# Copies of queries and keys within their own partitions: VectorE instead of transfers

## The chip, the cores and the metric

The kernel runs on one core of a Trainium2 chip. The metric is the device time of one execution in microseconds (us); lower is better. The engines of the core are TensorE (PE), VectorE (DVE), ScalarE (ACT), GpSimd (POOL) and SyncE (SP). SP issues all transfers (DMAs) of this kernel; the 16 DMA engines carry them out.

## The reference

The kernel computes a trunk of two layers over 2048 tokens of width 1024. Each layer normalizes its input, projects it to eight groups of 512 columns, runs two mixers side by side, gates and joins them, and projects back. The change concerns the queries and keys of the first mixer, chunked softmax attention with 8 heads of 64.

```python
def hybrid_layer(x, norm_gain, w_in, w_out, rel_bias, cos, sin):
    hn = rms_norm(x, norm_gain)
    proj = hn @ w_in.astype(hn.dtype)
    aq, ak, av, ag, rq, rk, rv, rg = jnp.split(proj, cuts, axis=-1)
    ya = chunked_rel_attention(aq, ak, av, rel_bias)      # 8 heads x 64, own chunk and 8 before
    yr = chunkwise_retention(rq, rk, rv, cos, sin)        # 4 heads x 128, recurrent state
    y = jnp.concatenate([ya * silu(ag), yr * silu(rg)], axis=-1)
    return x + y @ w_out

# in chunked_rel_attention, per chunk of 64 queries and its band of 576 keys:
    scores = jnp.einsum("bnqhd,bnkhd->bnhqk", qc, kb) * (dh ** -0.5)
    p = jax.nn.softmax(scores + bias, axis=-1)
    out = jnp.einsum("bnhqk,bnkhd->bnqhd", p, vb)
```

After the two layers comes a final RMS norm.

## The kernel before

**Numbers in two halves.** Matmul operands are f16. To keep more than f16's precision, a value is held as an upper half (the value rounded to f16) and a lower half (what the rounding left). ScalarE makes the upper half, VectorE the lower half by one subtraction. A projection is three matmul passes: upper by upper, upper by lower, lower by upper.

**Blocks.** A layer has four head groups `s` (two attention heads and one retention head each) and four stretches `n` of 512 tokens: 16 blocks a layer, 32 in all. A block first runs `dense_T` and then `dense_V`. `dense_T` computes four sections `j`, each 128 columns by 512 tokens with the columns on the partitions, in 24 matmuls of 512 columns (line 870; in the very first block lines 851 and 870): j = 0 attention queries, 1 attention keys, 2 and 3 the queries and keys of retention. `dense_V` computes four tiles of 128 tokens (line 891) with values and gates. Beside these matmuls run the attention and retention of the block before, in small portions between groups of eight matmuls: score matmuls (lines 939 and 940), the reduction of the scores on VectorE (943), exponential and upper half on ScalarE (946, 948), the lower half on POOL (949), a transposing transfer of both halves, `pT`, by SP (951), the product with the values (959 to 961), and retention products (999). The output projection of each layer (1289) follows after its 16 blocks.

**Queries and keys.** For j = 0 ScalarE writes the upper half of the queries into `qq[:, 0]` (line 767), and `q_rest` writes the lower half into `qq[:, 1]` (line 770). `qq` has the first head of the group on partitions 0 to 63 and the second on 64 to 127. The score matmuls contract over 128 partitions: on the key side 64 hold the upper half and 64 the lower half of one head, so each head's queries have to stand twice, on both halves of the partitions. `st.q[:, hx]` is that tile for head `hx`. `q_rest` fills it with four transfers (line 774), each of 64 partitions by 1024 f16 values. For j = 1 the same happens with `kk` (lines 781, 784): `k_rest` makes `st.k` by four transfers (lines 785 to 788) of 64 partitions by 512 values. In each set, two transfers keep the partitions of their source, and two move to the other half.

**Buffers.** `st.q` has two buffers and `st.k` three; `qq` and `kk` have one each, and these are used again in the same block for the rotation of the retention keys and queries. Dense products land in two PSUM tiles in turn (`psD`), the scores in one (`psS`), and the small products in four (`psR`).

**Order.** The order on PE, ACT, DVE and POOL is the order in which the program issues its instructions. It is written out by hand: `run` steps a block's matmuls in rounds, and each step may put work off by a number of rounds (`later`, with the table `PLACES`; ties go by `RANK`); `soon` puts `q_rest` and `k_rest` off in that way. In the very first block `soon` runs them at once, and the list `FIRST` orders the whole start: there the two evacuations stand directly ahead of the step `Vsc2`, which computes the scale (lines 1425 to 1433) for two sections of the V weights; ScalarE then converts these (1495) and VectorE makes their lower halves (1498). `PLAN` places the preparation of later tokens: squares, gain product on POOL (333, 1382), rounding on ScalarE (303), subtraction on VectorE (309), and two transposing transfers (312, 313). Of SP's queue only the start has a written order; after it, a planner places the transfers by estimated costs and due times.

Of the kernel before, what the change touches and what calls it, by code (L numbers as in the profile page):

```python
# [93 lines left out]
def hybrid_trunk(ctx: ExitStack, tc: tile.TileContext, x, pos, gain, gcol, w_in, w_out, rel, fgain,  # L94
# [9 lines left out]
    act, dve, pool, pe, sp = nc.scalar, nc.vector, nc.gpsimd, nc.tensor, nc.sync  # L104
# [580 lines left out]
    def later(k, fn, kind=None):  # L685
        if kind is not None:
            k = G(kind, k)
        if k <= 0:
            fn()
            return  # L690
        deferred.append([k, fn, kind])
# [16 lines left out]
    def dense_T(l, s, n, g, st):  # L708
# [12 lines left out]
        def soon(fn):  # L721
            if first:
                fn()
            else:
                later(1, fn, fn.__name__)

        def first_rotation(j, ps, rot):
            if j == 2:
                st.rq = rot
                later(1, tab_load)  # L730
                own = rot[:, 1:3].rearrange("p a c -> p (a c)").bitcast(F32)
            else:
                st.rk = rot
                own = b1.tile([P, 512], F32, tag="qq", name=f"raw{nm}")
            st.swp = []

            def cosine():
                dve.scalar_tensor_tensor(out=own, in0=ps, scalar=2.0 ** -16, in1=st.tabc, op0=ALU.mult, op1=ALU.mult)

            def sine(half):  # L740
                if half == 0:
                    st.swp = b1.tile([P, 512], F32, tag="swp", name=f"swp{nm}_{j}")
                i_, o_ = slice((1 - half) * 64, (2 - half) * 64), slice(half * 64, half * 64 + 64)
                dve.scalar_tensor_tensor(out=st.swp[o_], in0=ps[i_], scalar=-2.0 ** -16, in1=st.tabs[i_], op0=ALU.mult,
                                         op1=ALU.mult)

            def tokens():
                st.kt = b1.tile([P, KT, P], F16, tag="ktok", name=f"kt{nm}")
                sp.dma_start_transpose(out=st.kt, in_=rot.rearrange("p a c -> p (a c)"))

            d = 2 * j
            later(d, cosine)
            later(d, lambda: sine(0))
            later(d + 1, lambda: sine(1))
            later(d + 2, lambda: dve.tensor_tensor(own, own, st.swp, op=ALU.add))
            later(d + 3, lambda: act.activation(rot[:, 0], own, AF.Copy))
            later(d + 4, lambda: dve.tensor_tensor(rot[:, 1], own, rot[:, 0], op=ALU.subtract))
            if j == 2:
                later(d + 5, lambda: act.activation(rot[:, 2], rot[:, 0], AF.Copy, scale=2.0 ** -11))
            else:  # L760
                later(d + 6, tokens)

        def evacuate(j, ps):
            if j == 0:
                st.q = b2.tile([P, 2, 2, 512], F16, tag="q", name=f"q{nm}")
                qq = b1.tile([P, 2, 512], F16, tag="qq", name=f"qq{nm}")
                act.activation(qq[:, 0, :], ps, AF.Copy, scale=2.0 ** -16)

                def q_rest():
                    dve.scalar_tensor_tensor(out=qq[:, 1, :], in0=ps, scalar=2.0 ** -16, in1=qq[:, 0, :], op0=ALU.mult,  # L770
                                             op1=ALU.subtract)
                    for hx in range(2):
                        for half in range(2):
                            sp.dma_start(st.q[half * 64:half * 64 + 64, hx], qq[hx * 64:hx * 64 + 64])

                soon(q_rest)
            elif j == 1:
                st.k = b3.tile([P, 2, 512], F16, tag="k", name=f"k{nm}")
                kk = b1.tile([P, 2, 512], F16, tag="swp", name=f"kk{nm}")
                kh, kl = kk[:, 0, :], kk[:, 1, :]  # L780
                act.activation(kh, ps, AF.Copy, scale=2.0 ** -16)

                def k_rest():
                    dve.scalar_tensor_tensor(out=kl, in0=ps, scalar=2.0 ** -16, in1=kh, op0=ALU.mult, op1=ALU.subtract)
                    sp.dma_start(st.k[0:64, 0, :], kh[0:64, :])
                    sp.dma_start(st.k[64:128, 1, :], kh[64:128, :])
                    sp.dma_start(st.k[64:128, 0, :], kl[0:64, :])
                    sp.dma_start(st.k[0:64, 1, :], kl[64:128, :])

                soon(k_rest)  # L790
            else:
                w = 5 - j
                rot = b2.tile([P, w, 512], F16, tag=f"rot{j}", name=f"rot{nm}_{j}")
                if first:
                    first_rotation(j, ps, rot)
                    return
                if j == 2:
                    raw = rot[:, 1:3].rearrange("p a c -> p (a c)").bitcast(F32)
                else:
                    raw = b1.tile([P, 512], F32, tag="qq", name=f"raw{nm}")  # L800
                act.activation(raw, ps, AF.Copy, scale=2.0 ** -16)

                def swap(rot=rot, raw=raw, j=j):
                    swp = b1.tile([P, 512], F32, tag="swp", name=f"swp{nm}_{j}")
                    sp.dma_start(swp[0:64, :], raw[64:128, :])
                    sp.dma_start(swp[64:128, :], raw[0:64, :])

                    def turned(out_, x_, y_, op):
                        return lambda: dve.tensor_tensor(out_, x_, y_, op=op)

                    def upper():
                        act.activation(rot[:, 0], raw, AF.Copy)

                    def lower():
                        dve.tensor_tensor(rot[:, 1], raw, rot[:, 0], op=ALU.subtract)

                    def third():
                        act.activation(rot[:, 2], rot[:, 0], AF.Copy, scale=2.0 ** -11)

                    def tokens():  # L820
                        st.kt = b1.tile([P, KT, P], F16, tag="ktok", name=f"kt{nm}")
                        sp.dma_start_transpose(out=st.kt, in_=rot.rearrange("p a c -> p (a c)"))

                    d = 4 if j == 2 and first else 3
                    later(d, turned(raw, raw, st.tabc, ALU.mult), None if first else f'ro0{j}')
                    later(d + 1, turned(swp, swp, st.tabs, ALU.mult), None if first else f'ro1{j}')
                    later(d + 2, turned(raw, raw, swp, ALU.add), None if first else f'ro2{j}')
                    later(d + 3, upper, None if first else f'ro3{j}')
                    later(d + 4, lower, None if first else f'ro4{j}')
                    if j == 2:  # L830
                        later(d + 5, third, None if first else 'ro52')
                    else:
                        later(11, tokens, 'tok')

                if j == 2:
                    st.rq = rot
                    swap()
                    if first:
                        later(1, tab_load)
                else:  # L840
                    st.rk = rot
                    later(2, swap, 'sw')

        if first:
            ps = [psD.tile([P, 512], F32, tag="dense", name=f"dT{nm}_{j}") for j in range(2)]
            for (j, a) in ((0, 0), (0, 1), (0, 2), (1, 0), (1, 1), (1, 2), (0, 3), (1, 3)):
                cs = slice(a * P, (a + 1) * P)
                m = 0
                for (w_, h_) in ((g.h, hh), (g.h, hl), (g.l, hh)):
                    for kt in range(KT):  # L850
                        pe.matmul(ps[j][:, cs], w_[:, j, kt, :], h_[:, kt, cs], start=(m == 0), stop=(m == 23))  # L851
                        m += 1
                yield
            for j in range(2):
                evacuate(j, ps[j])
                yield
# [696 lines left out]
    for l in range(DEPTH):  # L1553
        gO = [Grp(), Grp()]
        go = Grp()
        for s in range(NSW):
            g = grp(l, s)
            for n in range(NS):
                first = (l, s, n) == (0, 0, 0)
                if not first:  # L1560
                    st = states.setdefault((l, s, n), St())
                    dT = dense_T(l, s, n, g, st)
                else:
                    st = st0
# [129 lines left out]
```

## Time and profile before

| what | value |
| --- | --- |
| median of 3 runs | 2025.08 us (2023.61 to 2025.53) |
| the profiled execution | 2026.06 us |
| its span, first to last instruction | 2024.3 us |
| granted TensorE clock, mean | 0.998 |
| busy: PE, DVE, ACT, POOL | 1987.4, 1298.6, 1157.4, 464.6 us |
| DMA queue of the kernel, share of 16 engines | 67.5% |
| transfers into `st.q` | 128, median 2.4 us from issue to landing |
| transfers into `st.k` | 128, median 2.0 us from issue to landing |

How to read the lines below: a row of a timeline gives the start in us from the span's start, the duration in us, the engine, the line of the kernel, the operation, output and input tiles by name, the shape, and a count; in brackets stands the idle time of the engine just before, with what ended it. A row of waits gives who waited for whom, the total in us, how often, and the longest. "PEld" is the loading of weights into TensorE, "SPq" the issuing of a transfer by SP. A matmul row lasts longer than the distance to the next one, since matmuls are pipelined.

### The profile page before, as it was taken

The numbers are of one execution on the slowest core, as the hardware profiler recorded it, in microseconds if no ns is written. First come the engines' busy times: TensorE is split into PE (matmuls) and PEld (weight loads), VectorE is DVE, ScalarE is ACT, GpSimd is POOL, SyncE is SP. The second block draws the span as 40 slices with busy tenths as digits, with TensorE's granted clock in tenths as the row PEclk, the third lists the DMA queues.
The fourth block names the chain that finished last, engine by engine and source line by source line (L and its number), as shares of the span: only waits on it lengthen the run. The fifth ranks groups of instructions, "written<-read, shape, count | busy, mean of one in ns | idle before, by whom it ended". The sixth has DMA issues, their size and how long they took to land.

```text
span 2024.3 us, 39702 instructions
## 1 busy us (share of the span) xinstructions
PE 1987.4 (98%) x14006; PEld 1047.4 (52%) x14006; DVE 1298.6 (64%) x4014; ACT 1157.4 (57%) x2525; POOL 464.6 (23%) x521
## 2 busy tenths in 40 slices
PE   6999999999999999999999999999999999999998
PEld 5444555555555555544444555555555555555544
DVE  7777767566656665766655557665766676557543
ACT  7666765566666655655445556655665665456432
POOL 2443222222222222220001222222212222222100
PEclk9999999999999999999999999999999999999999
DMA  9698765466586754899973547554755776558874
GB/s 269 137 187 191 159 145 123 105 144 127 131 186 139 148 135 101 187 244 266 236 183 94 119 97 163 121 119 102 162 119 132 168 163 161 119 123 185 208 206 125
DMA packets 655385, 315.25 MB, mean 156 GB/s; under 512 B 468784, under 2 KB 612144, under 8 KB 655184
## 3 DMA queue, kind: packets, MB, share of 16 engines
q1 hardware_dynamic: 655184, 312.70, 67.5%
q8 instruction: 110, 1.80, 0.4%
q14 instruction: 91, 0.75, 0.1%
HBM read 123.26 MB, written 41.98 MB: 82 GB/s over the span
## 4 chain that ended last, share of the span: by engine, by line
PE 89%; DMA 4%; DVE 4%; issue 1%; ACT 1%; SPq 1%; POOL 0%; POOLq 0%; ACTq 0%; DVEq 0%
PE dT L870 31%; PE dV L891 30%; PE dO L1289 13%; PE r L999 4%; PE S L940 3%; PE S L939 3%; DMA pT<-pq 2%; PE o L959 2%; PE o L960 2%; PE o L961 2%; PE dT L851 1%; DVE sc L943 0%; DMA x_d<-hTl 0%; DMA yly<-rly 0%; DMA xa<-in_x_dram 0%
## 5 line engine op out<-in xcount | busy, mean ns | idle before, releaser
L949 POOL TENSOR_TENSOR pq<-sc,pq 128x640 f16<-128x640 f32 (+4 forms) x256 | 329.3, 1286 | 1169.8 <-issue 710.3
L946 ACT ACTIVATE sc<-sc,mq,cT 128x640 f32<-128x640 f32 (+4 forms) x256 | 218.4, 853 | 427.7 <-DVE mq L945 427.6
L891 PE MATMUL dV<-whV,hTh 128*128 128x512 f16 x1024 | 352.1, 380 | 0.9 <-DVE gt L909 0.9
L891 PE MATMUL dV<-wlV,hTh 128*128 128x512 f16 x1024 | 352.2, 380 | 0.0
L891 PE MATMUL dV<-whV,hTl 128*128 128x512 f16 x1024 | 352.1, 379 | 0.0
L870 PE MATMUL dT<-hTh,whT 128*128 128x512 f16 x1008 | 346.6, 379 | 0.8 <-DMA hTh<-hTl 0.8
L870 PE MATMUL dT<-hTl,whT 128*128 128x512 f16 x1008 | 346.6, 379 | 0.0
L870 PE MATMUL dT<-hTh,wlT 128*128 128x512 f16 x1008 | 346.6, 379 | 0.0
L943 DVE CUSTOM_DVE_ANT_0 sc<-S,bias 128x640 f32<-128x640 f32 (+4 forms) x256 | 188.7, 737 | 197.9 <-PE S L940 196.8
L891 PEld LDWEIGHTS <-hTh 128*128 128x128 f16 x2048 | 196.6, 98 | 209.7 <-DVE gt L909 1.9
L870 PEld LDWEIGHTS <-whT 128*128 128x128 f16 x2016 | 192.5, 98 | 199.0 <-DVE gt L909 1.3
L948 ACT ACTIVATE pq<-sc 128x640 f16<-128x640 f32 (+4 forms) x256 | 171.5, 670 | 8.1
L1289 PE MATMUL dO<-whO,yly 128*128 128x512 f16 (+2 forms) x456 | 171.2, 376 | 1.5 <-DMA yly<-rly 1.5
L1289 PE MATMUL dO<-whO,yhy 128*128 128x512 f16 (+2 forms) x456 | 171.5, 377 | 0.5 <-DMA yhy<-rhy 0.5
L1289 PE MATMUL dO<-wlO,yhy 128*128 128x512 f16 (+2 forms) x456 | 171.5, 377 | 0.0
L891 PEld LDWEIGHTS <-hTl 128*128 128x128 f16 x1024 | 99.3, 98 | 104.3 <-issue 0.8
L870 PEld LDWEIGHTS <-wlT 128*128 128x128 f16 x1008 | 97.2, 98 | 100.6
L939 PE MATMUL S<-k,q 128*128 128x128 f16 (+3 forms) x592 | 142.1, 266 | 0.4 <-DVE mq L943 0.4
L1289 PEld LDWEIGHTS <-yhy 128*128 128x128 f16 x912 | 88.7, 98 | 102.4 <-issue 1.1
L959 PE MATMUL o<-v,pT 128*128 128x65 f16 x1120 | 129.1, 193 | 10.5 <-DMA pT<-pq 6.6
L940 PE MATMUL S<-k,q 128*128 128x128 f16 (+3 forms) x592 | 129.6, 267 | 0.0
L960 PE MATMUL o<-v,pT 128*128 128x64 f16 x1120 | 129.4, 194 | 0.0
(374 smaller groups left out, 3387.7 us busy)
## 6 DMA issues: line engine op xcount, KB each, us to landing
q<-qq SPq DMA_DIRECT2D x128, 128.0 KB, 2.4
yyy<-y_d SPq DMA_DIRECT2D x32, 512.0 KB, 4.6
stT<-in_w_in_dram SPq DMA_DIRECT2D x56, 256.0 KB, 3.6
stV<-in_w_in_dram SPq DMA_DIRECT2D x52, 256.0 KB, 3.4
k<-kk SPq DMA_DIRECT2D x128, 64.0 KB, 2.0
tabc<-tab SPq DMA_DIRECT2D x32, 256.0 KB, 2.7
tabs<-tab SPq DMA_DIRECT2D x32, 256.0 KB, 2.7
y_d<-yr SPq DMA_DIRECT2D x128, 64.0 KB, 2.0
```

What stands on the lines that cost most here:

```text
L870: pe.matmul(ps, w_[:, j, kt, :], h_[:, kt, :], start=(m == 0), stop=(m == 23))
L891: pe.matmul(ps, h_[:, kt, a * P:(a + 1) * P], w_[:, kt, :], start=(m == 0), stop=(m == 23))
L939: pe.matmul(o, st.q[:, hx, 0, cs], k_, start=True, stop=False)
L940: pe.matmul(o, st.q[:, hx, 1, cs], k_, start=False, stop=True)
L943: dve.tensor_tensor_reduce(out=v, in0=S[:, 0:w], in1=g.bias[hx][:, 640 - w:640], scale=1.0, scalar=-3.0e38, op0=ALU.add, op1=ALU.max, accu ...
L946: act.activation(v, v, AF.Exp, bias=m[:, 0:1], scale=g.c[:, 0:1])
L948: act.activation(pq[:, 0:w], v, AF.Copy)
L949: pool.tensor_tensor(pq[:, w:2 * w], v, pq[:, 0:w], op=ALU.subtract)
L959: pe.matmul(o[:, 0:65], u.p[:, b, :], v_[:, 0:65], start=(b == 0), stop=False)
L960: pe.matmul(o[:, 0:64], u.p[:, b, :], v_[:, 65:129], start=False, stop=False)
L999: pe.matmul(out_, w_, m_, start=(i == 0), stop=(i + 1 == len(pairs)))
L1289: pe.matmul(ps, h_[:, kt, :], w_[:, kt, c0:c1], start=(m == 0), stop=(m == 23))
```

## The change

The two transfers of each set that keep their partitions become copies on VectorE, issued in the same step as the subtraction: in `q_rest` each copy follows the transfer for the same head, in `k_rest` both copies follow the two transfers that are left. The transfers that move to the other half stay. This holds in all 32 blocks: 128 of the 256 transfers into `st.q` and `st.k` go, and 128 copies are added, 64 of 64 partitions by 1024 values and 64 of 64 by 512.

```diff
                     for hx in range(2):
-                        for half in range(2):
-                            sp.dma_start(st.q[half * 64:half * 64 + 64, hx], qq[hx * 64:hx * 64 + 64])
+                        own, other = (slice(64 * i, 64 * i + 64) for i in (hx, 1 - hx))
+                        sp.dma_start(st.q[other, hx], qq[own])
+                        dve.tensor_copy(st.q[own, hx], qq[own])
...
                     dve.scalar_tensor_tensor(out=kl, in0=ps, scalar=2.0 ** -16, in1=kh, op0=ALU.mult, op1=ALU.subtract)
-                    sp.dma_start(st.k[0:64, 0, :], kh[0:64, :])
-                    sp.dma_start(st.k[64:128, 1, :], kh[64:128, :])
                     sp.dma_start(st.k[64:128, 0, :], kl[0:64, :])
                     sp.dma_start(st.k[0:64, 1, :], kl[64:128, :])
+                    dve.tensor_copy(st.k[0:64, 0, :], kh[0:64, :])
+                    dve.tensor_copy(st.k[64:128, 1, :], kh[64:128, :])
```

## The prediction

> **What bounds the kernel now.** I read the page first, then the waits of TensorE by stretch, then one settled block and the first 75 us on each engine.
>
> ```profile
> PE 1987.4 (98%) x14006; PEld 1047.4 (52%) x14006; DVE 1298.6 (64%) x4014; ACT 1157.4 (57%) x2525; POOL 464.6 (23%) x521
> ...
> 270.00:850.00 580.00, 580.00 (x4331) 311.26 (x4329) 371.15 (x1235) 341.53 (x782) 141.29 (x157) 1.00 0.62 135
> ...
> 930.00:1900.00 970.00, 969.80 (x6826) 508.83 (x6824) 613.17 (x1913) 553.60 (x1228) 208.54 (x239) 1.00 0.65 150
> ```
>
> The first row counts busy time by engine. The other two are stretches: length, then busy time of PE, PEld, DVE, ACT and POOL, clock, DMA share, GB/s. From 270 to 850 us TensorE has no gap at all, from 930 to 1900 us it has 0.2 us. In these 1550 us nothing that VectorE or a transfer does is on the path; only a cover that breaks would be. What can move lies elsewhere, above all between 60 and 270 us, whose largest waits are:
>
> ```profile
> PE o L959 <- DMA pT<-pq: 3.2, 4, 1.4
> PE o L959 <- DVE rl L965: 2.5, 1, 2.5
> PE o L959 <- DVE yr L1064: 1.2, 1, 1.2
> PE dV L891 <- DVE gt L909: 0.9, 2, 0.5
> PE dT L870 <- DMA hTh<-hTl: 0.8, 1, 0.8
> ```
>
> These are total, count, longest: 8.6 us in nine waits, and VectorE ends several of them.
>
> **The settled block.** There are 32 blocks (two layers, four head groups, four stretches of 512 tokens); each loses four of its eight transfers and gains four VectorE copies.
>
> ```profile
> q<-qq SPq DMA_DIRECT2D x128, 128.0 KB, 2.4
> k<-kk SPq DMA_DIRECT2D x128, 64.0 KB, 2.0
> ...
> L774 SPq DMA_DIRECT2D q<-qq x128: 462/589/1801, 41.3 to 1798.5; - x128
> ...
> 392.03 0.69 DVE L770 SCALAR_TENSOR_TENSOR qq<-dT,qq 128x512 f16<-128x512 f32 x1 [1.78 <-ACT qq L767]
> 394.24 0.83 DVE L943 CUSTOM_DVE_ANT_0 sc<-S,bias 128x640 f32<-128x640 f32 x1 [1.52 <-PE S L940]
> ...
> 398.38 0.69 DVE L784 SCALAR_TENSOR_TENSOR kk<-dT,kk 128x512 f16<-128x512 f32 x1 [1.95 <-ACT kk L781]
> 398.99 0.28 DVE L1047 SCALAR_TENSOR_TENSOR state<-r,state 128x128 f32<-128x128 f32 x1
> 401.00 0.82 DVE L943 CUSTOM_DVE_ANT_0 sc<-S,bias 128x640 f32<-128x640 f32 x1 [1.72 <-PE S L940]
> ```
>
> Removed: two q and two k issues a block, of about 0.59 us each on SP's queue (the median of line 774), 2.4 us in all, and half of the bytes of the first two rows. SP is on no path of the settled stretch, so this is worth nothing there.
>
> Added: two copies of 64 partitions x 1024 f16 and two of 64 x 512. No copy of f16 within SBUF stands in the trace, so I bound it:
>
> ```profile
> 60.88 0.29 DVE L164 TENSOR_SCALAR xa<-xa 128x256 f32<-128x256 f32 x1
> ...
> 67.12 0.42 DVE L160 SCALAR_TENSOR_TENSOR xa<-xa 128x256 f32<-128x256 f32 x1
> ...
> 41.22 0.15 DVE L1425 TENSOR_REDUCE m2sV<-ms 128x1 f32<-128x2 f32 x1
> ```
>
> A nearly empty instruction takes 0.15 us. With one input 256 elements add 0.14 us, with two inputs 0.27 us. Per element at the one-input rate, the q copy is 0.15 + 4 x 0.14 = 0.71 us and the k copy 0.43 us. If bytes count and not elements, f16 halves the moving part: 0.43 and 0.29 us. The worst is the two-input rate: 1.23 and 0.69 us; the least is 0.15 us each. I take the middle of the two one-input readings, 0.57 and 0.36 us, because the row is f32 and the copy f16: 1.86 us a block, 60 us of VectorE's 2024. The Trainium skill, page "VectorE: DVE Perf Modes", section "The perf-mode tier table (the rule you actually need)", gives a 16-bit copy within SBUF four elements a cycle; an estimate from it is 0.42 and 0.28 us, and the first-block sum below would be 2.6 us by it instead of 3.0.
>
> The cover: behind the q subtraction VectorE sits idle for 1.52 us before the next score reduction (L943), against 1.14 us of copies; behind the k subtraction only the state update (L1047) stands, and then 1.72 us of idle against 0.72 us. So the reduction of the scores, which frees the one PSUM tile of the scores, isn't late. The buffers that the copies write were last read by the attention two stretches earlier, which is drained; nothing new is waited for. If the idle were gone, the queue behind would be L943 and after it ScalarE's exponential, POOL's difference and the transposed pT: 1.1 us late. Cost taken: nothing.
>
> **The first block.** Here the copies stand in a full VectorE queue, and POOL is busy beside them.
>
> ```profile
> 40.02 0.68 DVE L770 SCALAR_TENSOR_TENSOR qq<-dT,qq 128x512 f16<-128x512 f32 x1
> 40.62 0.68 DVE L784 SCALAR_TENSOR_TENSOR kk<-dT,kk 128x512 f16<-128x512 f32 x1
> ...
> 40.34 2.35 POOL L333 TENSOR_TENSOR hTh<-hTh,gb 128x1024 f32<-128x1024 f32 x1 [21.17 <-DMA tab<-wk]
> 46.37 2.56 POOL L333 TENSOR_TENSOR hTh<-hTh,gb 128x1024 f32<-128x1024 f32 x1 [3.68 <-ACT hTh L324]
> ...
> 46.85 2.17 DVE L441 TENSOR_SCALAR msk<-msk,rdc 128x128 f32<-128x128 f32 x1
> ...
> 42.02 2.19 ACT L1495 ACTIVATE whV<-hTl,sc2V 128x1024 f16<-128x1024 f32 x2 [1.76 <-DVE sc3V L1432]
> ...
> 53.21 0.28 ACT L899 ACTIVATE v<-dV 128x128 f16<-128x128 f32 x1 [0.98 <-PE dV L891]
> ...
> 55.56 0.29 DVE L905 SCALAR_TENSOR_TENSOR v<-dV,v 128x128 f16<-128x128 f32 x1 [1.83 <-ACT rv L901]
> ```
>
> The row of L441 shows a hold: 128 elements, less than L164's 256 at 0.29 us, take 2.17 us and end at 49.02, just behind the POOL product that runs from 46.37 to 48.93. A one-input VectorE instruction in SBUF waits until such a POOL product is over. The first q copy comes at 40.70, inside POOL's 40.34 to 42.69. So: 42.69, plus two q copies (1.14), the k subtraction (0.68) and two k copies (0.72), is 45.23. L1425, which starts the scale of the V weights, began at 41.22: it is 4.0 us late. ScalarE waited for that scale at 42.02, so its queue is 4.0 us late as well, and it has 0.98 us in hand before it has to evacuate the first dV (53.21). That leaves 3.0 us. VectorE waits for ScalarE at 55.56, with nothing in hand on that side, and goes 3.0 us later into the stretch that TensorE waits for:
>
> ```profile
> 56.02 0.41 DVE L909 SCALAR_TENSOR_TENSOR gt<-gt,dV 128x256 f32<-128x256 f32 x1
> ...
> 63.56 0.41 DVE L909 SCALAR_TENSOR_TENSOR gt<-gt,dV 128x256 f32<-128x256 f32 x1
> ...
> 64.03 0.39 PE L891 MATMUL dV<-whV,hTh 128*128 128x512 f16 x1 [0.50 <-DVE gt L909]
> ...
> 65.19 1.40 SPq L313 DMA_TRANSPOSE hTl<-hTl  x1
> 66.70 1.24 SPq L312 DMA_TRANSPOSE hTh<-hTl  x1
> ...
> 70.22 1.89 PE L870 MATMUL dT<-hTh,whT 128*128 128x512 f16 x8 [0.83 <-DMA hTh<-hTl]
> ```
>
> L909 frees a PSUM tile for the next dV but one; the transpose issued at 65.19 needs VectorE's work just before it, the one at 66.70 stands behind it in SP's queue, and dT at 70.22 waits for its landing. All of this moves by 3.0 us, and TensorE, without a gap from 270 us on, can't win it back there. SP's four saved issues don't help: SP is idle before these transposes, which wait for data. In the next three blocks the copies can again meet POOL products and wait for the rest of one, at most the 2.35 us of the row at 40.34. What stands behind them there is a score reduction, with a whole unit of attention until its use, and not a dV; I take nothing and keep 2.35 us for the range.
>
> The profiled execution took 2026.06 us, a span of 2024.3 and 1.8 around it; the median of the runs is 2025.08, 1.0 less. The sum is 2026.06 + 3.0 = 2029.1, so on the median **2028.1 us**, 0.15% slower. Changes under 0.2%, 4.05 us here, are what a measurement of this kernel can't tell from none.
>
> **Rivals.** (1) Slower beyond 0.2%: the wait at the fourth dV makes TensorE slow for a while. The rows for it:
>
> ```profile
> 208.51 5.18 PE dV L891 x24
> ...
> 164.91 0.20 PE L959 MATMUL o<-v,pT 128*128 128x65 f16 x1 [2.49 <-DVE rl L965]
> ...
> 166.62 0.63 PE L891 MATMUL dV<-whV,hTh 128*128 128x512 f16 x1
> 167.04 0.63 PE L891 MATMUL dV<-whV,hTl 128*128 128x512 f16 x1
> ...
> 169.34 0.38 PE L891 MATMUL dV<-whV,hTl 128*128 128x512 f16 x1
> 169.56 0.38 PE L891 MATMUL dV<-wlV,hTh 128*128 128x512 f16 x1
> ...
> 903.76 0.20 PE L959 MATMUL o<-v,pT 128*128 128x65 f16 x1 [1.92 <-DMA pT<-pq]
> ```
>
> The two L909 are 7.54 us apart and a dV of 24 matmuls lasts 5.18 (the row of 208.51), so once VectorE leads there, TensorE idles 2.36 us in one piece. After 2.49 us of idle the matmuls come every 0.42 us instead of 0.22, for about 3.4 us, which costs about 1.7 us. The fourth dV would then end at 63.97 + 5.18 + 1.7 = 70.85 plus the delay, 0.63 us behind dT's old start: 3.0 + 0.63 = 3.7 us. It passes 4.05 from a delay of 3.4 us, that is if a copy costs the per-element 0.71 and 0.43 us (3.45 + 0.63 = 4.1 us, 2029.2) or more (two-input rate: 5.0 + 0.63 = 5.6, 2030.7). For it: 2.36 lies close to 2.49. Against: 1.92 us stands in the trace without such a row that I could set beside it. The Trainium skill, "TensorE: Matmul & The Clock Gate", Part 1, puts the half clock after an idle window of about 3.4 us; by that rule 2.36 us cost nothing more and the sum stays 3.0. The row at 164.91 shows half rate after 2.49 us, so here the trace speaks for the rival.
>
> (2) Faster: SP's queue, 2.4 us a block shorter, brings the transposed pT earlier. At most the four pT waits (3.2 us), the wait at 164.91 (2.5) and its slow stretch (1.7) would go: 7.4 us, 2017.7. Against: these waits fall where SP waits for data as often as for its queue. More likely 1 to 2 us of it: 2023.5.
>
> (3) The change doesn't do what it says: the copy is ordered behind the transfer into the same tile, and VectorE stands still until that lands. The q transfer issued at 41.27 would land 2.4 us later; with the second one, and both k transfers 2.0 us after an issue near 46, the last copy ends near 49.1, L1425 is 7.9 us late, 6.9 beyond ScalarE's 0.98: 2032.0. Against: four transfers into one tile go out 0.6 us apart today, so writers of separate parts aren't ordered.
>
> **How the numbers follow.** Forecast 0.49 (a loss of 0.5 to 4 us); rival 1 beyond 0.2% 0.22, rival 3 0.06, and 0.06 for a new order of SP's queue, which a planner's costs set, with two more pT waits like the longest in the list (2 x 1.4 on top of 3.0): 2030.9. That is 0.34 slower. Rival 2 has 0.17, of which 0.09 beyond 0.2% and 0.08 within. So 0.09, 0.57, 0.34. With no hold and copies of the least 0.15 us the first block is 0.6 us late, hidden by the 0.98: 2025.1; with part of rival 2, 2023.5, the low end. The high end, 2032.0, takes in the two-input rate with the slow clock and rival 3.
>
> **What would show it.** Right: four copies a block, L774 and L785 to L788 with half their issues; TensorE busy for all of 270 to 850; the first copy near 40.7 lasting about 2.5 us; L1425 near 45, dT's start near 73.2 instead of 70.22. Wrong: the copy at 40.7 short (no hold); dT's start unmoved; new waits of TensorE on L943 or pT in the settled stretch; matmuls 0.42 us apart near 67 (rival 1); copies that end with a landing (rival 3).

## The result and the profile after

The changed kernel is slower: 2031.28 us (median of 6 runs, 2030.31 to 2032.87) against 2024.89 us for the kernel before (6 runs on the same chip, 2023.08 to 2026.33). The ratio is 1.003, with a 95% interval from 1.002 to 1.004, so about 6 us. The forecast was 2028.1 us in a range of 2023.5 to 2032.0: the side is right and the time lies in the range, but some 3 us of loss were not in the sum. The profiled execution after took 2031.73 us, span 2030.0 us, 5.7 us more than the span before.

First the busy times and the group of DMA issues that answer to the prediction's rows, from the page of the changed kernel:

```profile
PE 1989.6 (98%) x14006; PEld 1047.7 (52%) x14006; DVE 1353.2 (67%) x4142; ACT 1159.2 (57%) x2525; POOL 466.3 (23%) x521
...
q<-qq SPq DMA_DIRECT2D x64, 128.0 KB, 2.4
```

VectorE has 128 instructions more (4014 before) and is busy for 54.6 us more; the query transfers are half as many. So the change does what it says. The copies themselves, grouped by line (minimum, median and maximum of the duration in ns):

```profile
L775 DVE COPY q<-qq x64: 418/424/2232, 40.9 to 1801.3; 64x1024 f16<-64x1024 f16 x64
...
L788 DVE COPY k<-kk x32: 273/276/1454, 44.2 to 1807.9; 64x512 f16<-64x512 f16 x32
...
L789 DVE COPY k<-kk x32: 291/291/2406, 44.5 to 1808.2; 64x512 f16<-64x512 f16 x32
```

A copy costs 0.42 or 0.28 us, but the longest ones last 2.2, 1.5 and 2.4 us. In the whole trace only four of the 128 last over 1 us, at 40.9, 86.3, 134.6 and 141.8 us: one in the first block, one in the second, two in the third. A few more last 0.55 to 0.57 us.

Next TensorE's waits by what ended them (total, count, longest), between 60 and 270 us, to be set against the prediction's list for the same stretch:

```profile
PE o L960 <- DVE yr L1065: 4.7, 3, 2.6
PE dV L892 <- DVE gt L910: 3.2, 3, 2.2
PE o L960 <- DMA pT<-pq: 1.7, 1, 1.7
PE S L940 <- DVE mq L944: 1.7, 2, 1.3
```

The 8.6 us of that list became over 11 us, and all but 1.7 us of them now end on VectorE. The two stretches in which the prediction saw no gap:

```profile
270.00:850.00 580.00, 579.42 (x4321) 310.46 (x4319) 386.07 (x1281) 343.85 (x789) 142.09 (x158) 1.00 0.57 127
...
930.00:1900.00 970.00, 968.03 (x6803) 507.09 (x6801) 635.03 (x1972) 557.12 (x1232) 208.38 (x237) 1.00 0.64 143
```

In the first of them VectorE works 15 us more (371.15 before), the DMA share falls from 0.62 to 0.57, and TensorE is still busy for 579.4 of 580 us.

**The first block**, as the timeline of the changed kernel shows it (VectorE, POOL, ScalarE and TensorE rows put in order of time):

```profile
40.52 2.35 POOL L333 TENSOR_TENSOR hTh<-hTh,gb 128x1024 f32<-128x1024 f32 x1 [20.90 <-ACT hTh L324]
40.91 2.23 DVE L775 COPY q<-qq 64x1024 f16<-64x1024 f16 x1
...
43.61 0.69 DVE L785 SCALAR_TENSOR_TENSOR kk<-dT,kk 128x512 f16<-128x512 f32 x1
44.22 0.28 DVE L788 COPY k<-kk 64x512 f16<-64x512 f16 x1
...
44.83 0.16 DVE L1426 TENSOR_REDUCE m2sV<-ms 128x1 f32<-128x2 f32 x1
...
45.65 2.19 ACT L1496 ACTIVATE whV<-hTl,sc2V 128x1024 f16<-128x1024 f32 x2 [5.21 <-DVE sc3V L1433]
...
55.77 0.26 ACT L900 ACTIVATE v<-dV 128x128 f16<-128x128 f32 x1
...
66.58 0.61 PE L892 MATMUL dV<-whV,hTh 128*128 128x512 f16 x1 [2.19 <-DVE gt L910]
66.97 0.63 PE L892 MATMUL dV<-whV,hTl 128*128 128x512 f16 x1
...
69.53 0.59 PE L892 MATMUL dV<-whV,hTl 128*128 128x512 f16 x1
...
73.41 0.81 PE L871 MATMUL dT<-hTh,whT 128*128 128x512 f16 x3
```

The first query copy starts 0.4 us after POOL's product and ends 0.3 us behind it, at 43.14. The scale of the V weights (L1426) starts at 44.83 instead of 41.22, the first dV is evacuated at 55.77 instead of 53.21, and the fourth dV starts at 66.58, behind a wait of 2.2 us; for 3.4 us its matmuls then come 0.43 us apart instead of 0.22. dT starts at 73.41 instead of 70.22. Everything ahead of the change lies 0.18 us later in this execution (the subtraction of the queries at 40.20 instead of 40.02), so from that subtraction to dT it is 33.21 us instead of 30.20: 3.0 us lost.

**The third block** has two more of the long copies, the first q copy of 134.56 and the second k copy of 141.77. VectorE there before, and the same steps after:

```profile
130.25 0.68 DVE L770 SCALAR_TENSOR_TENSOR qq<-dT,qq 128x512 f16<-128x512 f32 x1
130.85 0.81 DVE L943 CUSTOM_DVE_ANT_0 sc<-S,bias 128x640 f32<-128x640 f32 x1
...
134.22 0.69 DVE L784 SCALAR_TENSOR_TENSOR kk<-dT,kk 128x512 f16<-128x512 f32 x1 [1.20 <-ACT kk L781]
...
137.38 0.82 DVE L943 CUSTOM_DVE_ANT_0 sc<-S,bias 128x640 f32<-128x640 f32 x1 [1.85 <-PE S L940]
...
140.01 1.27 DVE L309 SCALAR_TENSOR_TENSOR xa<-xin,rsn,xa 128x1024 f16<-128x1024 f32 x1
```


```profile
134.11 2.35 POOL L1383 TENSOR_TENSOR xin<-xin,gb 128x1024 f32<-128x1024 f32 x1
134.56 2.61 DVE L775 COPY q<-qq 64x1024 f16<-64x1024 f16 x2
137.21 0.82 DVE L944 CUSTOM_DVE_ANT_0 sc<-S,bias 128x640 f32<-128x640 f32 x1
...
141.20 0.55 DVE L788 COPY k<-kk 64x512 f16<-64x512 f16 x1
141.67 2.35 POOL L1383 TENSOR_TENSOR xin<-xin,gb 128x1024 f32<-128x1024 f32 x1
141.77 2.41 DVE L789 COPY k<-kk 64x512 f16<-64x512 f16 x1
144.20 0.29 DVE L1048 SCALAR_TENSOR_TENSOR state<-r,state 128x128 f32<-128x128 f32 x1
...
144.59 0.82 DVE L944 CUSTOM_DVE_ANT_0 sc<-S,bias 128x640 f32<-128x640 f32 x1
...
147.22 1.28 DVE L309 SCALAR_TENSOR_TENSOR xa<-xin,rsn,xa 128x1024 f16<-128x1024 f32 x1
...
162.14 0.27 PE L940 MATMUL S<-k,q 128*128 128x256 f16 x1 [1.32 <-DVE mq L944]
167.56 0.39 PE L892 MATMUL dV<-whV,hTh 128*128 128x512 f16 x1 [0.58 <-DVE gt L910]
172.02 0.19 PE L960 MATMUL o<-v,pT 128*128 128x65 f16 x1 [2.56 <-DVE yr L1065]
```

Before, the score reduction (L943) stood right behind the query subtraction, without any idle time, and 1.85 us of idle time stood ahead of the next one. After, the two q copies (2.61 us) and the two k copies (0.55 and 2.41 us) stand ahead of these reductions, the 1.85 us are gone, and L309, a step of the preparation of later tokens, starts 7.2 us late.

The order of TensorE's 14006 matmuls is the same before and after, so the same matmul can be looked up in both profiles. TensorE is 3.2 us late at dT, 4.1 us at the product that stood at 136.16, and 7.1 us at the one that stood at 172.79; at the last matmul it is 5.7 us late.

### The profile page after: what moved, and what is told of

The parts are those of the page before. It is cut to its first block, busy times and chain, and to the rows that moved or that the text cites. A ratio compares the mean times of both kernels' runs of the same rounds, so it can differ in the third digit from the quotient of the medians.

```text
span 2030.0 us, 39607 instructions
## 1 busy us (share of the span) xinstructions
PE 1989.6 (98%) x14006; PEld 1047.7 (52%) x14006; DVE 1353.2 (67%) x4142; ACT 1159.2 (57%) x2525; POOL 466.3 (23%) x521
## 4 chain that ended last, share of the span: by engine, by line
PE 81%; DMA 4%; DVE 4%; ACT 2%; issue 1%; SPq 1%; POOL 0%; ACTq 0%; POOLq 0%; DVEq 0%
PE dT L871 28%; PE dV L892 27%; PE dO L1290 12%; PE r L1000 4%; PE S L941 3%; PE S L940 3%; DMA pT<-pq 2%; PE o L960 2%; PE o L961 1%; PE o L962 1%; DVE sc L944 1%; DMA yly<-rly 1%; DMA stO0m<-in_w_out_dram 0%; ACT sc L947 0%; DMA x_d<-hTl 0%
```

## The experiments

Theory 1 was that single copies in the first blocks, which wait for the rest of a POOL product, make the loss. Its rivals were that some 54 us more VectorE work cost a little in each of 32 blocks, that the plain time of the copies counts and not the hold, and that a new order of SP's queue does it. All times below are medians; the kernel before, run beside them on the same chip, took 2025.96 us in the first set of four, 2024.83 in the second and 2025.37 in the third. Single executions of one kernel differ by some 7 us here, so the ratio with its interval counts.

**Where the loss lies.** The first four kernels take the copies back in some blocks, where the four transfers a set stand as before; the diff shows it for the queries, and the keys go the same way.

```diff
+                    if (l, s, n) == (0, 0, 0):    # e1; e2: (0, 0, 2); e3: (l, s) == (0, 0); e4: (l, s) != (0, 0)
+                        for hx in range(2):
+                            for half in range(2):
+                                sp.dma_start(st.q[half * 64:half * 64 + 64, hx], qq[hx * 64:hx * 64 + 64])
+                    else:
...
```

The first block:

> The first block (layer 0, group 0, stretch 0) by four and four transfers as before, the copies in the 31 others. Theory 1 (the loss comes from single copies in the first blocks that wait for a product of POOL, and 3.2 us of it stand at the first block's V sections): dT's start stays at 70.2 us, no matmuls 0.42 us apart near 67, and the time is about 2028 us, 3.2 below the change. Theory 2 (some 54 us more of VectorE's work cost about 0.2 us in each of 32 blocks): about 2031.1 us. Theory 3 (a new order of SP's queue): nothing changes at 66 us, and the total is anywhere within a few us.

Measured: 2028.99 us, ratio 1.0013 (1.0004 to 1.0021). dT starts at 70.60, 30.18 us behind the subtraction as before, and no slow matmuls follow.

The third block:

> Only the third block (layer 0, group 0, stretch 2), whose four copies of 134 to 144 us stand beside POOL products, by transfers as before. Theory 1: the steps of 136 to 165 us in TensorE's delay (3.1 to 7.3 us) go, the delay stays at about 3.2 us, and the time is 2027.5 to 2028.5 us. Theory 2: 2031.1 us.

Measured: 2027.18 us, ratio 1.0011 (1.0002 to 1.0019); dT late by 3.1 us, and the wait of 1.3 us on the score reduction near 160 us is gone. But TensorE's delay didn't stay at the expected 3.2 us: it is 4.5 us at 136.16 and 4.7 us at 172.79.

The first four blocks:

> The first four blocks (layer 0, group 0) by transfers as before, the copies in the 28 others, where all but a few copies last 0.42 and 0.28 us. Theory 1: 2024 to 2025.5 us, the time before, and TensorE starts dT at 70.2 us and is not late at 270 us. Theory 2: 28 times 0.2 us above the time before, 2030.5 us. If what SP's queue has less to do were worth something, this run shows it: below 2024 us.

Measured: 2026.51 us, ratio 1.0007 (0.9998 to 1.0016), not told apart from the kernel before, though 1 us above the top of the expected range: 28 of 32 blocks have the copies, and they cost nothing that shows (the interval leaves room for 3 us). It isn't below 2024 us either: SP's relief is worth nothing that shows.

The other way round:

> The copies in the first four blocks alone, transfers as before in the 28 others. Theory 1: the whole loss, about 2031 us, reached before 270 us. Theory 2: 4 times 0.2 us, 2025.7 us.

Measured: 2031.69 us, ratio 1.0028 (1.0019 to 1.0036). Four blocks of 32 carry the whole loss. The even spread of theory 2 is out: it asked for 2030.5 and 2025.7 us in the last two. By e1 and e2 the first and the third block each account for about half, but roughly: what is left of the loss is 0.8 to 4.3 us in the one and 0.4 to 3.8 us in the other.

The profile of this kernel shows something else in the first block, where its copies are those of the change (TensorE's timeline):

```profile
66.57 0.39 PE L903 MATMUL dV<-whV,hTh 128*128 128x512 f16 x1 [2.19 <-DVE gt L921]
66.79 0.38 PE L903 MATMUL dV<-whV,hTl 128*128 128x512 f16 x1
...
72.45 1.90 PE L882 MATMUL dT<-hTh,whT 128*128 128x512 f16 x8 [0.53 <-DVE gt L921]
```

TensorE waits 2.19 us at the fourth dV, as long as with the change, but here no slow matmuls follow: they come 0.22 us apart (the granted clock from 68 to 70 us is 1.00 here and 0.51 with the change), and dT starts 32.23 us behind the subtraction, 2.0 us late instead of 3.0. The profiles of e9 and e10 (further down) show the same: a wait of 2.19 us, no slow matmuls, dT 2.1 us late. That of e2 shows the wait with the slow matmuls, and dT 3.0 us late. So with the same copies the first block costs 2.0 to 2.1 us in some executions and 3.0 us in others.

**Hold or plain time.** Two kernels keep all transfers as before and put something else in the copies' places; their output tile is a scratch column.

```diff
-                        dve.tensor_copy(st.q[own, hx], qq[own])
+                        dve.tensor_copy(warm.bitcast(F16)[own], qq[own, 0, 0:2])                          # e5
+                        dve.tensor_reduce(warm[own], qq[own, 0, 0:256], axis=AX.X, op=ALU.max)            # e6
...
+                        dve.tensor_copy(warm.bitcast(F16)[own], kh[own, 0:2])                             # e5
+                        dve.tensor_reduce(warm[own], kh[own, 0:128], axis=AX.X, op=ALU.max)               # e6
```

Copies of next to nothing:

> All four transfers a set as before, and in the places of the copies VectorE copies of 64 partitions by 2 f16 values into a scratch column: next to no time of their own, but of the same kind. Theory 1 (the hold by POOL's products): the copy at about 41 us still lasts until POOL's product ends, L1425 is 2.3 to 2.6 us late, the third block's copies hold the score reduction too, and the time is 2027.5 to 2030 us. Rival (the plain time of the copies): four times 0.15 us, nothing is late beyond ScalarE's 0.98 us, and the time is that of before, 2024.5 to 2026 us.

Measured: 2028.18 us, ratio 1.0014 (1.0006 to 1.0023). In the groups by line and the timeline of this kernel:

```profile
L777 DVE COPY warm<-qq x64: 149/168/2085, 40.7 to 1797.2; 64x2 f16<-64x2 f16 x64
...
40.40 2.34 POOL L333 TENSOR_TENSOR hTh<-hTh,gb 128x1024 f32<-128x1024 f32 x1 [21.14 <-ACT hTh L324]
40.68 2.28 DVE L777 COPY warm<-qq 64x2 f16<-64x2 f16 x2
```

A copy of two values a partition lasts 0.17 us, and beside POOL 2.09. It makes dT 2.3 us late (72.60, 32.52 us behind the subtraction), and the slow matmuls come too. So the hold alone makes most of the first block's loss. Its third block has a held query copy of 2.03 us, but a pair of key copies of 0.61 us, and loses little; more on that below.

Plain time without a hold:

> All four transfers a set as before, and in the places of the copies VectorE reductions of 64 partitions by 256 and by 128 f16 values to a scratch column: plain time of about the copies' 0.42 and 0.28 us, but not a copy. Theory 1, if a reduction isn't held: all of them last 0.2 to 0.45 us, also beside POOL's products, L1425 is 1.1 to 1.4 us late, and the time is 2024.5 to 2026.5 us. Rival (plain time): about 2031 us, as with the change. If the reduction is held as well, its rows at 41 and 134 us show it (over 2 us), and the time is near 2031 us under both.

Measured: 2026.38 us, ratio 1.0008 (1.0000 to 1.0016).

```profile
L777 DVE TENSOR_REDUCE warm<-qq x64: 398/409/418, 40.0 to 1794.3; 64x1 f32<-64x256 f16 x64
...
39.97 0.85 DVE L777 TENSOR_REDUCE warm<-qq 64x1 f32<-64x256 f16 x2
```

No reduction of the 64 lasts longer than 0.418 us, though two of them run at 39.97 to 40.82 with POOL's product from 39.68 on. L1425's counterpart starts 2.70 us behind the query subtraction instead of 1.20, and dT 30.59 instead of 30.20 us: 0.4 us lost, what the 1.4 us of plain time leave over ScalarE's 0.98. The interval leaves room for up to 3 us of plain cost in the whole, but not for the 6 us of the change. The Trainium skill, page "SBUF — State Buffer", section "Who interferes with whom", says that VectorE's copies can take the second pair of ports, which it shares with GpSimd, and then the later of the two waits for the whole instruction, while a reduction on trn2 never does. These two runs agree: 2.09 us for the copy, 0.41 for the reduction at the same place.

**The same copies at other places.** The copies of the first three blocks go into gaps between POOL's products; nothing else differs from the change.

```diff
-"... d d Vsc2 Vhi3 Vhi2 ..."
+"... d d Vsc2 cp Vhi3 Vhi2 ..."      # first block: all four copies behind the scale (L1425 to L1433)
...
+    QP, KP = {(0, 0, 2): 2}, {(0, 0, 1): 2, (0, 0, 2): 1.5}      # rounds later: queries, keys
```

> The change, with its copies in the first three blocks put into gaps between POOL's products: in the first block all four behind the scale of the V weights (L1425 to L1433), where VectorE waits for ScalarE; in the second the key copies, in the third both sets some instructions later. Theory 1: no copy there waits long, L1425 starts at 41.2 to 41.4 us, dT at 70.2 to 70.5 us, and the time is 2024 to 2026.5 us. Theory 2 (54 us more of work): 2031 us. Below 2024 us only if SP's relief is worth something.

Measured: 2025.11 us, ratio 1.0004 (0.9995 to 1.0012). The loss is gone, with all 128 copies in place. VectorE's timeline in the first block:

```profile
40.64 0.15 DVE L1440 TENSOR_REDUCE m2sV<-ms 128x1 f32<-128x2 f32 x1
...
41.58 1.25 DVE L783 COPY q<-qq 64x1024 f16<-64x1024 f16 x2
42.84 0.28 DVE L799 COPY k<-kk 64x512 f16<-64x512 f16 x1
43.14 0.29 DVE L800 COPY k<-kk 64x512 f16<-64x512 f16 x1
43.67 2.48 DVE L1513 SCALAR_TENSOR_TENSOR wlV<-hTl,sc2V,whV 128x1024 f16<-128x1024 f32 x2 [0.24 <-ACT whV L1510]
```

The scale starts at once, the first copy still waits 0.4 us for POOL, and all four end in the 2.0 us for which VectorE had waited for ScalarE there; 0.24 us of that is left. With SP's four issues a block less and no copy held for longer than this one, the time is that of the kernel before.

A version with no copy at all (queries shown, keys alike):

```diff
-                act.activation(qq[:, 0, :], ps, AF.Copy, scale=2.0 ** -16)
+                for hx in range(2):
+                    act.activation(st.q[half[hx], hx, 0, :], ps[half[hx]], AF.Copy, scale=2.0 ** -16)
...
+                        dve.scalar_tensor_tensor(out=st.q[own, hx, 1, :], in0=ps[own], scalar=2.0 ** -16,
+                                                 in1=st.q[own, hx, 0, :], op0=ALU.mult, op1=ALU.subtract)
+                        sp.dma_start(st.q[other, hx], st.q[own, hx])
```

> No copy within SBUF: ScalarE writes the upper half of each head straight into its own partitions of the tile that the scores read (two instructions for one), VectorE subtracts head by head (two for one), and the transfers to the other half read from there; half of the transfers go as with the change. VectorE has about 1.2 us a block more, ScalarE about 1.0. Theory 1: nothing is held; L1425 is about 1.2 us late in the first block, 0.2 us beyond the 0.98 us in hand, and the time is 2024 to 2027 us. Theory 2 (about 40 us more VectorE's and 32 us more ScalarE's work): 2030 us or more.

Measured: 2028.38 us, ratio 1.0019 (1.0011 to 1.0028), above what theory 1 allowed. Its profile (span 2023.1 us) fell on the fastest of its 11 executions, at 2024.99 us, and TensorE ends 1.1 us earlier there than before. So this profile can't show what the others lose; that stays open. As a way to do without the hold it is worse than moving the copies.

**Which copy in the third block.** Two kernels give one of the two sets back to the transfers there.

```diff
+                    if (l, s, n) == (0, 0, 2):    # in e9 around the queries' set, in e10 around the keys'
+                        for hx in range(2):
...
+                    else:
...
```

> The change, but in the third block (layer 0, group 0, stretch 2) the queries by transfers as before and only the keys by copies. The profile of the change shows there one held query copy of 2.2 us and a held pair of key copies of 3.0 us. Theory A (the key copies make the third block's loss, since the state update and the score reduction that TensorE's next waits name stand behind them): TensorE's delay grows from 3.1 us at 136 us to about 6 us by 170 us, with a wait on L943's successor near 156 us, and the time is about 2030 to 2031 us, unless the earlier place of the copies lets them miss POOL's product, which their rows would show. Theory B (the query copy makes it): the delay stays near 3.2 us, 2028 us.

Measured: 2028.57 us, ratio 1.0016 (1.0007 to 1.0025). The key copies are held again, and the rows are:

```profile
137.40 0.55 DVE L793 COPY k<-kk 64x512 f16<-64x512 f16 x1
137.97 2.40 DVE L794 COPY k<-kk 64x512 f16<-64x512 f16 x1
...
169.84 0.23 PE L965 MATMUL o<-v,pT 128*128 128x65 f16 x1 [4.13 <-DVE rl L971]
```

> The change, but in the third block the keys by transfers as before and only the queries by copies. Theory A (the key copies make the third block's loss): the query copy at 134 us still lasts 2.2 us, TensorE's delay stays near 3.2 us from 136 to 170 us, and the time is about 2028 us. Theory B (the query copy): the delay grows to 6 us or more by 170 us, 2031 us.

Measured: 2029.50 us, ratio 1.0024 (1.0015 to 1.0033). Here is how late TensorE is at the same matmul, in us against the profile of before, worked out from the start times in the two traces. The columns are the matmul's start before; "start" is how late the first block's query subtraction is, ahead of all copies, and "growth" is the growth between dT and 172.79.

```
                            start    70.22   136.16   172.79   growth   270.0   last matmul
change                       0.17     3.20     4.07     7.07     3.9     5.85      5.68
e1 first block back          0.41     0.39     2.02     4.29     3.9     3.93      5.67
e4 first four only           0.20     2.24     3.10     6.12     3.9     4.55      5.79
e9 third block: keys        -0.23     1.88     3.27     5.65     3.8     3.94      2.33
e10 third block: queries    -0.56     1.52     3.24     3.54     2.0     3.42      4.65
e2 third block back          0.07     3.12     4.51     4.75     1.6     3.56      2.90
e3 first four back          -0.64    -0.70     0.79     1.15     1.9     1.19     -0.46
e5 tiny copies               0.06     2.38     3.05     3.77     1.4     2.62      2.02
e6 reductions               -0.66    -0.26     1.10     0.29     0.6     0.16     -1.99
e7 in gaps                  -0.58    -0.87    -0.17    -1.10    -0.2    -1.02     -1.62
e8 no copies                -0.92    -0.48     1.67     1.65     2.1     2.07     -1.14
```

With held key copies in the third block the delay grows by 3.8 to 3.9 us, in four of four profiles; without, by -0.2 to 2.1 us, and that has nothing to do with copies in the third block, since e3 and e8 have none there. This speaks for the key copies (theory A), but two things speak against reading it as their price. Behind the longest wait of this stretch the matmuls come at half rate (0.43 us apart) for a while in the profile of before and in most others, but not in e2, e6, e7 and e10, whose growth is the smaller for it. And the difference doesn't last. At 270 us, less the start, the change (both sets) is 5.7 us late and e2 (neither) 3.5, both with the slow matmuls in the first block; e4 (both) is 4.4 us late, e9 (keys) 4.2 and e10 (queries) 4.0, all three without them. So both sets together cost about 2.2 us in the third block (1.7 us by e1 against e3), and which of the two does it is not settled. The whole times don't separate them either: e10 is not faster than e9, and neither came out where theory A put it. What comes after 172 us differs from profile to profile: e9 gets 3.3 us back and e10 loses 1.1, in waits on pT near 584, 889 and 910 us and in stretches at half rate near 910 and 927 us. How much of the third block's loss is still there at the end is therefore not settled.

The held key copy of the second block (86.3 us) costs nothing that shows: from dT to 136.16 the delay grows by 0.9 us with the change, and by 1.5 us in e3, which has no copies there.

**How far the cover reaches.**

```diff
+                        for _ in range(3):
                             dve.tensor_copy(st.q[own, hx], qq[own])
```

> The first four blocks by transfers as before; in the 28 others the copies, each made three times: about 4.2 us of copies a block instead of 1.4, 78 us more VectorE work in all than with the change. Behind the query subtraction 2.5 us of copies stand against 1.52 us of idle time, so the score reduction is 1.0 us late there; behind the key subtraction 1.7 us against 1.72. Theory 1 (the transposed pT has some us in hand in most units, so that the settled blocks pay nothing even beyond the idle time of VectorE): 2025 to 2030 us. Rival (the settled blocks pay what goes beyond VectorE's idle time): 28 times 1.0 us, 2053 us.

Measured: 2043.38 us, ratio 1.0086 (1.0072 to 1.0100), between the two: 18 us for 118 us of added VectorE work (28 blocks of 4.2 us). TensorE's waits in 270 to 850 us name another place than either theory:

```profile
PE dV L905 <- ACT whV L422: 2.8, 2, 1.4
PE msT L415 <- DVE mbT L403: 1.4, 2, 0.7
PE o L973 <- DMA pT<-pq: 0.7, 1, 0.7
```

The late score reductions of this stretch show as one wait of 0.7 us on pT. What TensorE waits for is the preparation of the next head group's weights, once or twice a group: its scale stands in VectorE's queue behind the key copies, and ScalarE's conversion (L422) behind the scale. The copies made once fit ahead of it, the same made three times don't.

## Why the prediction was right and wrong

**Settled blocks, nothing: right.** e3 shows it with the copies in 28 blocks, within its interval of 3 us. That the copies of a settled block are hidden behind idle VectorE was the right reason, but the step that said what would be late without the cover named the wrong work: not the score reduction and pT, but the weights at the change of a group (e11).

**SP's relief, nothing: right.** Rival 2 (2023.5 us or less) would have shown in e3 and e7, where the copies do no harm. Both are level with the kernel before; their intervals leave room for a gain of 1 us at most.

**Price of a copy: too high.** The sum took 0.57 and 0.36 us, the middle of two readings; measured are 0.42 and 0.28, a little below its lower reading (0.43 and 0.29) and equal to the estimate from the Trainium skill, page "VectorE: DVE Perf Modes", section "The perf-mode tier table (the rule you actually need)". The trace of before had no row that could decide it.

**The hold: right.** The copy at 40.91 waits for POOL's product as L441 had done; e5 and e6 show that it is the kind of instruction that waits and not its size.

**The first block, 3.0 us: right in size, by errors that cancel and by luck.** L1426 came 3.6 us late by the clock and 3.4 against the subtraction, not 4.0, since the copies are shorter. After ScalarE's 0.98 us that leaves 2.4 us (55.77 and 66.58 show it). Then rival 1's slow clock set in behind the fourth dV's wait of 2.2 us, as the row at 164.91 had suggested, and brought it back to 3.0: 2.4 plus its price of 0.63. So rival 1's mechanism happened inside the forecast, below its own threshold. The last step of the path is another one too: the forecast let dT wait for the landing of a transpose, as before; in this profile dT waits for nothing, and it is TensorE itself that comes late (the row of 73.41). That the two agree is luck: in e4, e9 and e10 no slow clock follows the same wait, and the loss is 2.0 to 2.1 us. The Trainium skill's rule of about 3.4 us ("TensorE: Matmul & The Clock Gate", Part 1) would have had an idle time of 2.2 us cost nothing; the rows from 66.97 to 69.53 disagree, and e4's rows agree with it.

**The next three blocks, nothing: this step failed.** The prediction saw that a copy could meet a POOL product there and kept 2.35 us for the range; it argued that only a score reduction stands behind the copies, with a unit of attention in hand. But the cover that it had worked out for a settled block, 1.52 us of idle time behind the query subtraction, isn't there in the third: before, the reduction stood right behind that subtraction (130.25 and 130.85). And the copies were held three times and not once: 2.17 us for a query copy, then 0.55 and 2.41 us for the key copies, by two products in turn, against the 1.85 us of idle time ahead of the next reduction (137.38). So VectorE came 7.2 us late to L309 (147.22 against 140.01; in e2, without these copies, 4.5), and TensorE's delay grew by 3.9 us to 172.79, of which e3, without copies there, has 1.9; by e2, about 2 us of loss are left of it at 270 us. In whole times, taking the third block's copies back saved about half of the loss (e2). With the first block's 2 to 3 us that makes most of the 6 us; the rest lies within the intervals. SP's order (the last rival) isn't needed: e7 has the same transfers, and they cost nothing.

## What to carry to other kernels

An added instruction on an idle engine costs what it holds up, not what it takes: look which other engine it shares something with at its place in the queue, and what stands behind it. Here copies of 0.3 to 0.4 us lasted 1.5 to 2.4 us four times in 128, and the loss came from two of the three blocks in which they did; moving the copies of three blocks to places where they aren't held for long undid it. When a cover is claimed, check it at each place where it is needed: the idle time of a settled block isn't that of the start. And look for the rare chain that uses the same engine (a change of weights), not only for the one that runs all the time.

## What the runs showed of the hardware

- A VectorE copy of 64 x 2 f16 values, 0.17 us alone, took 2.09 us when it started 0.3 us after a POOL product of two f32 inputs (128 x 1024) that lasts 2.34 us, and ended just behind it. A reduction of 64 x 256 f16 at the same place kept its 0.41 us. The POOL product kept its 2.35 us.
- Shorter POOL products hold a copy too: the 64 x 512 copies of 0.55 us at 141.20 and, in e9, at 137.40, and those of 0.55 to 0.57 us now and then in later blocks. There POOL paid too: its small instruction behind the product (L1061) lasted 0.80 us at 194.90, 347.03 and 604.39 us instead of 0.55.
- Half rate (matmuls of 512 columns 0.43 us apart instead of 0.22) came behind some waits of TensorE and not behind others that were as long. It came behind 2.19 us in the change (3.4 us of it, from 66.58 to 69.96) and in e2, and behind 2.13 us in e5; it did not come behind 2.19 us at the same matmul in e4, e9 and e10, nor behind 3.26 us in e10 (169.45). What decides it besides the length of the wait is open.
